# Modulation vectors of a conditioned decoder trunk: the sum on VectorE's free axis in place of partition sums and transposes

## The chip, the cores and the metric

The kernel runs on one core of one Trainium2 chip. The metric is the device time of one execution in microseconds (us); lower is better. Three runs of the kernel before took 1095.26, 1096.6 and 1096.73 us; their median is 1096.6.

## The reference

Two layers work on x, 256 tokens by 1024. Each layer runs a half-step SwiGLU feed-forward (FFN), a token mixer, and a second FFN. Around each of the three, the input is normalised, scaled and shifted, and the output is gated, by vectors that depend on the sequence alone:

```
c_act = silu(c)                                  # c: 1024 numbers
for l in range(2):
    mod = c_act @ w_ada[l] + b_ada[l]            # w_ada[l]: 1024 x 9216
    sh0, sc0, g0, sh1, sc1, g1, sh2, sc2, g2 = split(mod, 9)
    h = rmsnorm(x, norm_g[l, 0]) * (1 + sc0) + sh0
    x = x + 0.5 * g0 * swiglu(h, gate, up, down) # 1024 -> 2816 -> 1024
    h = rmsnorm(x, norm_g[l, 1]) * (1 + sc1) + sh1
    x = x + g1 * token_mix(h, ...)
    h = rmsnorm(x, norm_g[l, 2]) * (1 + sc2) + sh2
    x = x + 0.5 * g2 * swiglu(h, ...)
return rmsnorm(x, final_g)
```

The token mixer is a gated unit, a differential attention and a sparse attention side by side, between an input and an output projection. The change touches how `mod` is computed. All inputs are float32.

## The kernel before, in words

The activations lie with the model axis on the partitions: xT is 128 partitions by 8 chunks by 256 tokens. A projection takes 128 output rows at a time. Its weights (`wst`, 128x1024, 512 KB) come in by DMA from SyncE's queue (SP) and are split in two parts for an exact product: ScalarE (ACT) copies the high part `wh` (L207), VectorE (DVE) subtracts for the rest `wl` (L211). TensorE (PE) multiplies wh by both parts of the activations and wl by one, three products for each of 8 chunks (L219). An FFN runs 22 gate/up tiles (`ps_ws`, two times 24 products each; but for the first FFN, the first two tiles start from x before its norm is known, `ps_wu`) and then 8 down tiles (`ps_dn`, 44 products). The mixer runs its parts in an order written out by hand (MIX_ORDER) for TensorE; elsewhere the framework's planner sets the order on each engine. Each engine runs its queue in order.

A modulation vector m of layer l (9 in each) is made in two halves of 512 columns. The first two vectors of layer 0 are made in the startup by another path (`ada_row`, `ada_col`, L362 to L383), which the change leaves as it is. The other 32 halves go through `ada_half` (L183): four loads of 512 KB on SP, each with 256 rows of the summed axis, two on each partition, by 512 columns; VectorE multiplies by the column of silu(c) and adds into `acc`, 128x512 (L192, L194). That leaves the sum over the 128 partitions, which `ada_flush` (L171) does one step later: four transposes on TensorE into one PSUM bank (L176), four copies on ScalarE that give the sum of each row (L180), and then the bias add and the gain or gate on VectorE (`ada_cols`, L158). The bank (pool `pst`, one buffer) is shared with the norms and the compressed branch. The load buffers (`ad`, four of 4 KB a partition) are shared with the compression weights.

The callers set where halves run (L1016 to L1036): 4 during the gate/up tiles and 4 during the down tiles of the first FFN, 4 in the first mixer (steps `a` of MIX_ORDER and the output projection), 6 and 2 in the next FFN, 6 and 4 in layer 1's first FFN, none in its mixer, and 2 in the last FFN. The first FFN begins with `startup` (L356), where seven gate/up tiles are built up chunk by chunk in seven PSUM banks while the first modulations arrive; it ends with the rest of the constants and parameters being loaded (L440, L441) and the Silu evictions of the seven tiles.

Of the kernel before, what the change touches and what calls it, by code (L numbers as in the profile page):

```python
# [10 lines left out]
F32 = mybir.dt.float32  # L11
# [6 lines left out]
P = 128  # L18
# [27 lines left out]
NW = 16         # products that warm the tensor engine while the first loads arrive  # L46
BUFS = dict(acc=2, ad=4, sm=4, t1k=9, u=27, wh=6, wl=6, wst=5)
LATE = 4        # tiles of the first FFN that run before it loads modulation weights
# order of the parts of the token mixer, layer by layer
# [9 lines left out]
NE = 2          # gate/up tiles (and pairs of w_in tiles) that run before the norm is known  # L59
NS = 7          # gate/up tiles of the first FFN that are accumulated while w_ada arrives  # L60
# [51 lines left out]
def trunk_kernel(ctx: ExitStack, tc: tile.TileContext, A, depth=DEPTH, nf=NF, fsplit=FSPLIT):  # L112
# [33 lines left out]
    nc.scalar.activation(cact, par[:, :8], AF.Silu)  # L146
    ones = sing.tile([P, 1], F32, name="ones")
# [21 lines left out]
    pending = []  # L169

    def ada_flush():  # L171
        while pending:
            l, m, hf, acc = pending.pop(0)
            ps = pst.tile([P, 512], F32, name="ps_ada", tag="st")
            for c in range(4):
                nc.tensor.transpose(ps[:, c * P:(c + 1) * P], acc[:, c * P:(c + 1) * P], ident)  # L176
            red = sm.tile([P, 4], F32, name="red", tag="red")
            for c in range(4):
                junk = tp.tile([P, P], F32, name="junk", tag="t1k")
                nc.scalar.activation(junk, ps[:, c * P:(c + 1) * P], AF.Copy, accum_out=red[:, c:c + 1])  # L180
            ada_cols(l, m, slice(hf * 4, hf * 4 + 4), red)

    def ada_half(l, m, hf):  # L183
        ada_flush()
        acc = accp.tile([P, 512], F32, name="acc")
        for q in range(4):
            st = adp.tile([P, 2, 512], F32, name="ast")
            nc.sync.dma_start(st, A["w_ada"][l, m, hf, q])
            for k2 in range(2):
                col = cact[:, 2 * q + k2:2 * q + k2 + 1]  # L190
                if q == 0 and k2 == 0:
                    nc.vector.tensor_scalar_mul(acc, st[:, 0, :], col)  # L192
                else:
                    nc.vector.scalar_tensor_tensor(out=acc, in0=st[:, k2, :], scalar=col, in1=acc,  # L194
                                                   op0=ALU.mult, op1=ALU.add)
        pending.append((l, m, hf, acc))

# [38 lines left out]
    # brings the table of Sqrt in behind an instruction  # L236
# [5 lines left out]
    # 1/rms of every token, broadcast over the partitions  # L242
# [36 lines left out]
    # x * gain before the norm is known: parts of a chunk, and the shift as two more columns  # L279
# [11 lines left out]
    # W^T (x * gain) and, per row, W^T shift  # L291
# [17 lines left out]
    # out[128 rows of W, T] of W^T h: weights stationary  # L309
# [45 lines left out]
    # the first gate/up tiles, chunk by chunk of the model axis as its modulation arrives  # L355
    def startup(ns):  # L356
# [84 lines left out]
        dma(par[:, npar0:], A["par"][:, npar0:])  # L441
        return [swiglu_mul(ps[:, :T], ps[:, T:], None, None, up, "u") for ps in pss]
# [7 lines left out]
    def ffn(l, w, ada_f, ada_d, nxt):  # L450
# [17 lines left out]
        for f in range(f0, nf):  # L468
            ada_flush()
            for args in slots.get(f - f0 - late, ()):  # L470
                ada_half(*args)
            pg = ws_in(gate[f], psm, "mm")
            pu = ws_in(upw[f], psm, "mm")
            act.append(swiglu(pg, pu))
            for _ in range(2):
                if raw:
                    n = f0 - len(raw)
                    act[n] = act_tile(raw.pop(0))
# [4 lines left out]
        for m in range(KD):  # L483
            ada_flush()
            for args in slots.get(m, ()):
                ada_half(*args)
            if m == KD - 2:
                ada_flush()
                sqrt_table(after)
                if nxt is not None:  # L490
                    u_shift(*nxt)
            ps = psm.tile([P, 2 * T], F32, name="ps_dn", tag="mm")
            final = nxt is None and m == KD - 1
            f0_ = 0
            for n in fsplit:
                wh, wl = split(A["w_down"][l, w, m, :, f0_ * P:(f0_ + n) * P], n * P)
                for j in range(n):
                    f = f0_ + j
                    if final:
                        for n3, (wx, rhs) in enumerate(((wh, act[f][:, :T]), (wh, act[f][:, T:]), (wl, act[f][:, :T]))):  # L500
                            mm(ps[:, :T], wx[:, j * P:(j + 1) * P], rhs, f == 0 and n3 == 0, f == nf - 1 and n3 == 2)
                        continue
                    mm(ps, wh[:, j * P:(j + 1) * P], act[f], start=(f == 0), stop=False)
                    mm(ps[:, :T], wl[:, j * P:(j + 1) * P], act[f][:, :T], start=False, stop=(f == nf - 1))
                f0_ += n
            after = add_out(l, s, m, ps, nxt, 1 if final else 2)

# [22 lines left out]
    # exp of score segments [128, n, keys] in PSUM, with the sums of their rows  # L530
# [13 lines left out]
    def mix(l, ada, nxt):  # L544
# [10 lines left out]
        # lambda of the differential attention, on every partition  # L555
# [29 lines left out]
        # -- projections, tokens on partitions --  # L585
# [31 lines left out]
        # -- gate of the spatial gating unit (before the norm is known) --  # L617
# [8 lines left out]
        # -- blocks of the compressed branch: columns (group, block), position code, position code --  # L626
# [15 lines left out]
        # -- values of the differential attention, v of the gating unit --  # L642
# [22 lines left out]
        # -- differential attention --  # L665
# [93 lines left out]
        # -- spatial gating unit --  # L759
# [35 lines left out]
        # -- compressed keys and values --  # L795
# [40 lines left out]
        # -- sparse attention --  # L836
# [120 lines left out]
        def ada_next():  # L957
            ada_flush()
            if ada:
                ada_half(*ada.pop(0))  # L960
# [44 lines left out]
        ada_flush()  # L1005
        for m in range(2, KD):
            if ada:
                ada_next()
            if m == KD - 2:
                ada_flush()  # L1010
                sqrt_table(after)
                u_shift(*nxt)
            after = w_out(m, 0, KD)

# [66 lines left out]
def _layout(inp, depth, nf):  # L1081
# [5 lines left out]
    o["w_ada"] = g["w_ada"].reshape(depth, 4, 2, P, NMOD, 2, 512).transpose(0, 4, 5, 1, 3, 2, 6)  # L1087
# [54 lines left out]
```

## Time and profile before

| what | value |
|---|---|
| median of three runs | 1096.6 us |
| span of the profiled execution (the page gives no time around it) | 1093.7 us |
| PE busy | 1060.2 us, 97%, 7928 products |
| PE weight loads | 970.2 us, 89% |
| DVE busy | 850.8 us, 78%, 1573 instructions |
| ACT busy | 624.7 us, 57%, 1320 instructions |
| DMA | 257.55 MB, mean 235 GB/s |
| chain that ended last | PE 83%, DVE 10%, ACT 5%, issue 1%, DMA 1% |

Busy times are sums over one execution; engines run side by side. The span goes from the first to the last instruction. Products on PE are pipelined, so that their durations overlap: a product of 283 ns can follow the one before after less than half of that. The chain goes back from the last instruction to what released it, step by step, and shows which engine's work set the end.

### The profile page before, as it was taken

The page shows a single profiled execution, that of the slowest core. Times are in us where ns is not written, and L with a number is a line of the kernel's source. Part 1 is how long each engine was busy: PE and PEld are TensorE (multiplying, and loading weights), DVE is VectorE, ACT ScalarE, POOL GpSimd, SP SyncE. Part 2 cuts the span into 40 slices and gives each one's busy share as a digit, 9 for nine tenths or more (in the row PEclk, how much of TensorE's full clock was granted, in tenths as well). Part 3 has the DMA queues.
Part 4 walks back from the last instruction along what each step waited for, and adds up shares of the span by engine and source line. Part 5 has one row for each costly group of instructions (what it writes and reads, how often), then busy time and mean ns, then how long its engine had stood idle before and what let it go on. Part 6 is the DMA issues. An engine that isn't in the chain of part 4 may idle for free.

```text
span 1093.7 us, 20684 instructions
## 1 busy us (share of the span) xinstructions
PE 1060.2 (97%) x7928; PEld 970.2 (89%) x7928; DVE 850.8 (78%) x1573; ACT 624.7 (57%) x1320; POOL 0.2 (0%) x4
## 2 busy tenths in 40 slices
PE   8999999998988999999999999999999999999997
PEld 5899998887775999999899999988787699999986
DVE  3479999767997999887879878786799878555563
ACT  4365545666675865554556555455867766454441
POOL 0000000000000000000000000000000000000000
PEclk8999999999998999999999999999999999999999
DMA  8868988944835679997866888785555145555551
GB/s 330 295 238 339 355 326 310 324 160 132 320 130 181 221 243 343 341 312 252 280 230 231 318 277 297 263 312 197 180 184 184 58 154 174 188 180 187 174 159 39
DMA packets 73827, 257.55 MB, mean 235 GB/s; under 512 B 8320, under 2 KB 9728, under 8 KB 73728
## 3 DMA queue, kind: packets, MB, share of 16 engines
q1 hardware_dynamic: 73728, 256.23, 67.3%
q8 instruction: 62, 1.02, 0.4%
q14 instruction: 37, 0.30, 0.1%
HBM read 255.14 MB, written 1.05 MB: 234 GB/s over the span
## 4 chain that ended last, share of the span: by engine, by line
PE 83%; DVE 10%; ACT 5%; issue 1%; DMA 1%; SPq 0%; DVEq 0%; ACTq 0%
PE ps_ws L219 41%; PE ps_dn L219 23%; PE ps_wu L219 5%; PE ps_fst L219 4%; PE ps_out L219 4%; DVE wl L211 2%; DVE rt L512 2%; PE ps_y L219 1%; DVE mx L533 1%; ACT cmpa L637 1%; PE ps_ada L176 1%; PE ps_row L219 1%; DVE acc L194 1%; ACT pn L538 1%; DMA ast<-in_w_ada_dram 1%
## 5 line engine op out<-in xcount | busy, mean ns | idle before, releaser
L207 ACT ACTIVATE wh<-wst 128x1024 fp32r<-128x1024 f32 (+2 forms) x332 | 340.3, 1030 | 289.0 <-PE ps_ws L219 101.9
L219 PE MATMUL ps_ws<-h,wh 128*128 128x256 f32 x2720 | 488.9, 283 | 6.9 <-DVE dv L650 6.1
L211 DVE TENSOR_TENSOR wl<-wst,wh 128x1024 fp32r<-128x1024 f32 (+2 forms) x332 | 391.0, 1183 | 118.2 <-ACT wh L207 116.9
L219 PEld LDWEIGHTS ps_ws<-h,wh 128*128 128x128 f32 x2720 | 419.6, 190 | 9.2 <-DVE dv L650 7.0
L219 PE MATMUL ps_ws<-h,wl 128*128 128x256 f32 x1360 | 383.2, 282 | 0.3 <-DVE wl L211 0.3
L219 PEld LDWEIGHTS ps_ws<-h,wl 128*128 128x128 f32 x1360 | 258.0, 190 | 0.5 <-DVE wl L211 0.5
L219 PE MATMUL ps_dn<-act,wh 128*128 128x512 f32 (+1 forms) x726 | 249.1, 391 | 0.0
L219 PE MATMUL ps_dn<-act,wl 128*128 128x256 f32 x704 | 197.7, 281 | 0.0
L194 DVE SCALAR_TENSOR_TENSOR acc<-ast,cact,acc 128x512 f32<-128x512 f32 x224 | 167.3, 747 | 2.5
L219 PEld LDWEIGHTS ps_dn<-act,wh 128*128 128x128 f32 x726 | 134.9, 188 | 30.3
L219 PEld LDWEIGHTS ps_dn<-act,wl 128*128 128x128 f32 x704 | 133.2, 189 | 0.0
L219 PE MATMUL ps_wu<-ut,wh 128*128 128x258 f32 (+1 forms) x320 | 60.1, 286 | 0.9 <-DVE ut L288 0.9
L219 PEld LDWEIGHTS ps_wu<-ut,wh 128*128 128x128 f32 x320 | 49.7, 189 | 1.4 <-DVE ut L288 1.3
L342 DVE TENSOR_TENSOR a<-ps_ws,sg 128x256 f32<-128x256 f32 x75 | 31.6, 421 | 21.8 <-PE ps_ws L219 21.5
L219 PE MATMUL ps_out<-y,wh 128*128 128x256 f32 x256 | 47.4, 286 | 0.2 <-DVE xT L325 0.2
L215 ACT ACTIVATE act<-a 128x256 fp32r<-128x256 f32 x88 | 35.2, 408 | 21.1 <-DVE a L342 19.1
L219 PE MATMUL ps_fst<-h,wh 128*128 128x256 f32 x224 | 43.4, 297 | 1.8 <-ACT h L275 1.8
L219 PE MATMUL ps_wu<-ut,wl 128*128 128x258 f32 x160 | 45.0, 282 | 0.0
L219 PEld LDWEIGHTS ps_fst<-h,wh 128*128 128x128 f32 x224 | 35.5, 198 | 6.9 <-issue 4.5
L219 PEld LDWEIGHTS ps_out<-y,wh 128*128 128x128 f32 x256 | 39.8, 191 | 1.6 <-issue 1.0
L325 DVE SCALAR_TENSOR_TENSOR xT<-ps_dn,hg,xT 128x256 f32<-128x256 f32 x63 | 30.2, 480 | 12.0 <-PE ps_dn L219 11.3
L226 ACT ACTIVATE sq<-xT 128x256 f32<-128x256 f32 x48 | 19.9, 414 | 33.7 <-DVE xT L325 33.2
(203 smaller groups left out, 1115.1 us busy)
## 6 DMA issues: line engine op xcount, KB each, us to landing
ast<-in_w_ada_dram SPq DMA_DIRECT2D x144, 512.0 KB, 5.3
wst<-in_w_gate_dram SPq DMA_DIRECT2D x81, 512.0 KB, 4.5
wst<-in_w_up_dram SPq DMA_DIRECT2D x81, 512.0 KB, 4.3
wst<-in_w_down_dram SPq DMA_DIRECT2D x64, 512.0 KB, 4.5
wst<-in_w_in_ws_dram SPq DMA_DIRECT2D x28, 512.0 KB, 3.8
wst<-in_w_down_dram SPq DMA_DIRECT2D x32, 384.0 KB, 4.0
wst<-in_cmp_w_dram SPq DMA_DIRECT2D x16, 512.0 KB, 5.8
wst<-in_w_out_dram SPq DMA_DIRECT2D x16, 512.0 KB, 4.8
```

Source lines behind the costliest of these rows:

```text
L176: nc.tensor.transpose(ps[:, c * P:(c + 1) * P], acc[:, c * P:(c + 1) * P], ident)
L194: nc.vector.scalar_tensor_tensor(out=acc, in0=st[:, k2, :], scalar=col, in1=acc, op0=ALU.mult, op1=ALU.add)
L207: nc.scalar.activation(wh, st, AF.Copy)
L211: nc.vector.tensor_sub(wl, st, wh.bitcast(F32))
L215: nc.scalar.activation(dst[:, :T], src, AF.Copy)
L219: nc.tensor.matmul(out, lhsT, rhs, start=start, stop=stop, skip_group_check=True)
L226: square = nc.scalar.activation(sq, xT[:, k, :], AF.Square)
L325: nc.vector.scalar_tensor_tensor(out=xT[:, m, :], in0=ps[:, half * T:(half + 1) * T], scalar=hg[l][:, s, m:m + 1], in1=xT[:, m, :], op0=AL ...
L342: nc.vector.tensor_mul(a, pu, sg)
L512: nc.vector.tensor_mul(out, z, t)
L533: nc.vector.tensor_reduce(mx[:, :n], ps, axis=AX.X, op=ALU.max, negate=True)
L538: nc.scalar.activation(pt[:, g * w:(g + 1) * w], ps[:, g, :], AF.Exp, bias=mx[:, g:g + 1], accum_out=su[:, g:g + 1])
```

## The change

The weights w_ada are laid out so that the summed axis of 1024 lies along the free axis: a load of 512 KB now holds 128 modulations on the partitions and all 1024 rows of the sum beside each other. silu(c) is kept as a row on every partition (`crow`, 128x1024), loaded at the end of the startup and put through Silu there. For 128 modulations VectorE runs one instruction, which multiplies the weights by crow (in place) and gives the sum of each partition in one column of `red` (`accum_out`); four of them make a half, and ada_cols follows at once. `ada_flush`, the pending list, the acc tiles of 512 columns, the transposes and ScalarE's copies are gone. The host's layout of w_ada follows, and c is handed over on 128 partitions. Comments that the diff deletes are left out here.

```diff
@@ trunk_kernel
     nc.scalar.activation(cact, par[:, :8], AF.Silu)
+    crow = sing.tile([P, D], F32, name="crow")
...
-    pending = []
-
-    def ada_flush():
-        while pending:
-            l, m, hf, acc = pending.pop(0)
-            ps = pst.tile([P, 512], F32, name="ps_ada", tag="st")
-            for c in range(4):
-                nc.tensor.transpose(ps[:, c * P:(c + 1) * P], acc[:, c * P:(c + 1) * P], ident)
-            red = sm.tile([P, 4], F32, name="red", tag="red")
-            for c in range(4):
-                junk = tp.tile([P, P], F32, name="junk", tag="t1k")
-                nc.scalar.activation(junk, ps[:, c * P:(c + 1) * P], AF.Copy, accum_out=red[:, c:c + 1])
-            ada_cols(l, m, slice(hf * 4, hf * 4 + 4), red)
 
     def ada_half(l, m, hf):
-        ada_flush()
-        acc = accp.tile([P, 512], F32, name="acc")
-        for q in range(4):
-            st = adp.tile([P, 2, 512], F32, name="ast")
-            nc.sync.dma_start(st, A["w_ada"][l, m, hf, q])
-            for k2 in range(2):
-                col = cact[:, 2 * q + k2:2 * q + k2 + 1]
-                if q == 0 and k2 == 0:
-                    nc.vector.tensor_scalar_mul(acc, st[:, 0, :], col)
-                else:
-                    nc.vector.scalar_tensor_tensor(out=acc, in0=st[:, k2, :], scalar=col, in1=acc,
-                                                   op0=ALU.mult, op1=ALU.add)
-        pending.append((l, m, hf, acc))
+        red = sm.tile([P, 4], F32, name="red", tag="red")
+        for c in range(4):
+            st = adp.tile([P, D], F32, name="ast", tag="ast")
+            nc.sync.dma_start(st, A["w_ada"][l, m, hf * 4 + c])
+            nc.vector.scalar_tensor_tensor(out=st, in0=st, scalar=1.0, in1=crow, op0=ALU.mult, op1=ALU.mult,
+                                           accum_out=red[:, c:c + 1])
+        ada_cols(l, m, slice(hf * 4, hf * 4 + 4), red)
@@ startup
         dma(par[:, npar0:], A["par"][:, npar0:])
+        dma(crow, A["crow"])
+        nc.scalar.activation(crow, crow, AF.Silu)
         return [swiglu_mul(ps[:, :T], ps[:, T:], None, None, up, "u") for ps in pss]
@@ ffn, mix: every call of ada_flush() goes
...
@@ _layout
-    o["w_ada"] = g["w_ada"].reshape(depth, 4, 2, P, NMOD, 2, 512).transpose(0, 4, 5, 1, 3, 2, 6)
+    o["w_ada"] = g["w_ada"].reshape(depth, D, NMOD, KD, P).transpose(0, 2, 3, 4, 1)
+    o["crow"] = np.broadcast_to(g["c"][0], (P, D))
```

## Rows read from the trace of the kernel before

**Rows 1.** By stage: us, length, PE, PEld, DVE, ACT, POOL busy, clock, DMA, GB/s.
```profile
70.70:224.00 153.30, 152.99 (x1125) 144.65 (x1125) 138.49 (x210) 87.32 (x180) 0.00 (x0) 1.00 0.86 320
224.00:374.00 150.00, 136.34 (x979) 113.78 (x978) 126.85 (x314) 102.57 (x273) 0.00 (x0) 0.95 0.55 188
374.00:565.00 191.00, 191.00 (x1446) 182.58 (x1445) 164.03 (x259) 105.72 (x206) 0.00 (x0) 1.00 0.83 289
565.00:757.00 192.00, 192.00 (x1455) 183.61 (x1454) 158.72 (x252) 107.24 (x222) 0.00 (x0) 1.00 0.79 270
757.00:897.00 140.00, 133.38 (x979) 113.24 (x978) 115.95 (x289) 99.60 (x243) 0.00 (x0) 0.98 0.44 153
897.00:1086.00 189.00, 188.19 (x1453) 181.56 (x1451) 109.88 (x163) 90.92 (x146) 0.00 (x0) 1.00 0.49 159
```

**Rows 2.** The chain that ended last, its shares by line, whole kernel.
```profile
by line: PE ps_ws L219 41.1%; PE ps_dn L219 22.6%; PE ps_wu L219 4.9%; PE ps_fst L219 3.9%; PE ps_out L219 3.7%; DVE wl L211 1.9%; DVE rt L512 1.6%; PE ps_y L219 1.5%; DVE mx L533 1.4%; ACT cmpa L637 1.4%; PE ps_ada L176 1.3%; issue 1.2%; P
```

**Rows 3.** Chain pieces in feed-forward stages: start us, us, what.
```profile
99.66 0.44 PE ps_ada L176 x4
...
111.92 16.90 PE ps_ws L219 x144
...
915.77 56.32 PE ps_ws L219 x480
972.09 0.44 PE ps_ada L176 x4
```

**Rows 4.** PE timeline round one group of transposes: start us, us, engine, line.
```profile
110.85 0.28 PE L219 MATMUL ps_ws<-h,wl 128*128 128x256 f32 x1
...
111.21 0.28 PE L219 MATMUL ps_ws<-h,wl 128*128 128x256 f32 x1
...
112.00 0.28 PE L219 MATMUL ps_ws<-h,wl 128*128 128x256 f32 x1
```

**Rows 5.** Chain pieces of the transposes in the first mixer.
```profile
345.57 1.04 PE ps_ada L176 x4
...
355.71 0.44 PE ps_ada L176 x4
...
367.72 0.44 PE ps_ada L176 x4
```

**Rows 6.** Groups by line and form: busy us, mean ns | idle before.
```profile
L211 DVE TENSOR_TENSOR wl<-wst,wh 128x1024 fp32r<-128x1024 f32 x286 | 348.0, 1221 | 116.2 <-ACT wh L207 115.0
L207 ACT ACTIVATE wh<-wst 128x1024 fp32r<-128x1024 f32 x286 | 302.0, 1060 | 251.0 <-PE ps_ws L219 91.1 <-issue 84.9 <-PE ps_dn L219 47.1
...
L194 DVE SCALAR_TENSOR_TENSOR acc<-ast,cact,acc 128x512 f32<-128x512 f32 x224 | 167.3, 747 | 2.5
...
L180 ACT ACTIVATION_READ_ACCUMULATOR junk<-ps_ada 128x1 f32 x128 | 26.1, 204 | 0.0
...
L272 DVE SCALAR_TENSOR_TENSOR tn<-xT,gs,rb 128x256 f32<-128x256 f32 x48 | 20.8, 478 | 0.3
...
L192 DVE TENSOR_SCALAR acc<-ast,cact 128x512 f32<-128x512 f32 x32 | 15.4, 482 | 0.4 <-PE ps_ada L176 0.2 <-DMA ast<-in_w_ada_dram 0.2
...
L160 DVE TENSOR_TENSOR mod<-red,par 128x4 f32<-128x4 f32 x32 | 5.0, 157 | 1.3 <-ACT junk L180 1.2
```

**Rows 7.** DVE timeline in the first mixer: start us, us, engine, line.
```profile
288.05 0.74 DVE L194 SCALAR_TENSOR_TENSOR acc<-ast,cact,acc 128x512 f32<-128x512 f32 x1
288.71 1.22 DVE L211 TENSOR_TENSOR wl<-wst,wh 128x1024 fp32r<-128x1024 f32 x1
289.85 0.74 DVE L194 SCALAR_TENSOR_TENSOR acc<-ast,cact,acc 128x512 f32<-128x512 f32 x1
```

**Rows 8.** SP timeline at the end of the startup.
```profile
53.56 0.38 SPq L201 DMA_DIRECT2D wst<-in_w_gate_dram  x1
```

**Rows 9.** ACT timeline at the end of the startup.
```profile
66.68 0.39 ACT L337 ACTIVATE sg<-ps_fst 128x256 f32<-128x256 f32 x1 [1.09 <-PE ps_fst L219]
```

**Rows 10.** Waits, whole kernel: the largest of ACT for weights: us, times, longest.
```profile
ACT wh L207 <- DMA wst<-in_w_down_dram: 4.6, 4, 2.0
```

More of the change, by code (lines that the diff above doesn't have):

```diff
@@ L468, in ffn @@
         for f in range(f0, nf):
-            ada_flush()
             for args in slots.get(f - f0 - late, ()):
@@ L483, in ffn @@
         for m in range(KD):
-            ada_flush()
             for args in slots.get(m, ()):
@@ L487, in ffn @@
             if m == KD - 2:
-                ada_flush()
                 sqrt_table(after)
@@ L957, in ada_next @@
         def ada_next():
-            ada_flush()
             if ada:
@@ L1004, in mix @@
             steps[name](*map(int, args))
-        ada_flush()
         for m in range(2, KD):
@@ L1009, in mix @@
             if m == KD - 2:
-                ada_flush()
                 sqrt_table(after)
```

## The prediction

> **What bounds the kernel now.** I read the stages first, then the chain of waits, then single stretches. The stage table [rows 1] has one row per feed-forward (FFN) or mixer stage behind the startup, which fills the first 70.7 us. In the four FFN rows TensorE (first busy column) is busy for all but 0.3, 0, 0 and 0.8 us of the stage, at full granted clock. VectorE (third column) is the next engine: 138.5 of 153.3 us in the first FFN, 164.0 of 191, 158.7 of 192, 109.9 of 189. In the two mixers TensorE is idle for 13.7 and 6.6 us; the first, which carries modulation work, takes 150 us and the second 140. So in an FFN a microsecond of TensorE work is a microsecond of the kernel, as long as VectorE and the loads keep up; in the first mixer VectorE counts too.
>
> The chain [rows 2] has ps_ada L176, the transposes that the change removes, with 1.3% of 1093.7 us = 14.2 us. Its pieces in the FFNs are 0.44 us each [rows 3]; four transposes make one group. The chip's own order says the same: the two weight products before a group start 0.36 us apart (110.85, 111.21), the two around it 0.79 us (111.21, 112.00) [rows 4], so a group costs 0.43. And 480 weight products without a group take 56.32 us, 0.117 each; 144 between two groups take 16.90, again 0.117 [rows 3]: beside the gap the groups slow nothing.
>
> **Counting.** A half (512 modulations) is one group of four transposes. The code asks for 8 halves in the first FFN, 4 in the first mixer, then 8, 10 and 2 in the other FFNs: 32, of which 28 are in FFNs. 28 x 0.44 = 12.3, and the three groups of the first mixer that are on the chain have 1.04 + 0.44 + 0.44 = 1.9 [rows 5]; together 14.2, the chain's share.
>
> **The change part by part.**
>
> *TensorE.* 128 transposes go: -12.3 us in the FFNs, where nothing else is late by much (below), and -1.9 in the first mixer. The fourth mixer group is not on the chain: 0. The 16 transposes of the startup (L379) stay.
>
> *ScalarE.* 128 copies with sum from PSUM and their 128 accumulator reads (204 ns each [rows 6]) go. ScalarE is busy for 87 of 153 us in its fullest FFN [rows 1] and before its largest group, the copies of the weights (L207), it idles mostly for TensorE [rows 6], so 0. The one PSUM bank that they shared with the norms is free earlier; 0 too.
>
> *VectorE.* Before, a half is one product of 128x512 (482 ns) and seven products with add (747 ns) [rows 6]: 0.48 + 7 x 0.747 = 5.71 us. After, it is four products over 128x1024 that also give a sum. The trace has none with a sum on this engine. The same instruction takes 478 ns for 256 columns and 747 for 512 [rows 6], 1.05 ns a column, so 747 + 2 x 269 = 1285 ns for 1024. Reading the sum out I take as a small instruction of this engine, 157 ns [rows 6]. That gives 4 x (1.285 + 0.157) = 5.77 us, 0.06 more than before: no change. Bounds: from below the plain two-input subtraction of 128x1024, 1221 ns, with a read that hides wholly, 4.88 us a half, 0.83 less; from above twice the time a column, 747 + 512 x 1.05 + 1024 x 1.05 = 2.36 us, with ScalarE's read of 0.204, 10.3 us, 4.5 more. They lie far apart; I take the value next to the row of the same instruction, L194. In the FFNs +0.06 is hidden by VectorE's slack of 14.8 us or more [rows 1]. In the first mixer VectorE runs its instructions end to end, and each starts some 0.08 us before the one before it ends (288.05, 288.71, 289.85 against 0.74 and 1.22 long [rows 7]), for old and new alike: 4 halves x 0.06 = +0.2 us there, with bounds of -3.3 and +18.
>
> Here a rule speaks against the change. The row shows L194 with two f32 inputs and a scalar at 1.05 ns a column [rows 6]. The Trainium skill, "Vector Engine (DVE) Microarchitecture Reference", section "7. Points that are easy to get wrong", says that this instruction runs at half rate when both tensor sources lie in SBUF and are not bf16, since both read ports are then taken and none is left to read back the accumulator. By L194's row it does not hold for the instruction without a sum; no run here shows it with one. The sum by the rule is the second rival below.
>
> *Waits and order.* The bias add of a half now waits for VectorE's own sums alone, no longer for TensorE and ScalarE, and is not put off to the next step: it comes earlier, gain 0. A load buffer is free after one product of 1.2 us instead of two of 0.67: no later, so SP, on which the weight loads queue behind these loads, is not held longer. Bytes and pieces of the modulation loads are the same.
>
> *Startup.* New are one load of 512 KB (c on all partitions) and one Silu over 128x1024. The load is issued on SP ahead of the gate weights that go out at 53.56 [rows 8]; at the 320 GB/s of the next stage [rows 1] it holds them for 1.6 us, and they are not needed before 66.68, when the first tiles are evicted. The Silu waits for that load on ScalarE's queue with the seven Silu evictions behind it, which free the PSUM banks that TensorE needs next. It costs about the 1060 ns of the copy of that shape [rows 6], and ScalarE is idle for 1.09 us just there [rows 9]. So 0 to 1.6 + 1.06 = 2.7; I take 0.3, since both covers are larger than what they cover.
>
> **Sum.** -12.3 - 1.9 + 0.2 + 0.3 = -13.7 us: a span of 1093.7 - 13.7 = 1080.0. The page gives the profiled execution's span alone; the median of the three runs, 1096.6, is 2.9 above it. Forecast 1082.9 us, with 1079.1 (VectorE at its lower bound, -3.5 against its term, and no startup cost) to 1087.2 (startup at its upper bound, +2.4, and the 1.9 us of the mixer's groups not gained) for this case. **Chance 0.70.**
>
> **Rivals.**
>
> *The gain is handed back to VectorE or the loads.* With TensorE faster, the weights' split on VectorE or their loads end last in places. For: DMA share 0.86 and 0.83 in the first and second FFN, VectorE 90% in the first [rows 1]. Against: the largest wait of ScalarE for a weight load is 4.6 us in all over four times [rows 10], and TensorE never stands. If it takes back all 16 groups of these two stages, 16 x 0.44 = 7.0: 1090. **0.09.**
>
> *Half rate with a sum.* One mechanism: the product with sum takes 2.36 us, a half 4 x (2.36 + 0.157) = 10.1, 4.36 more than before. VectorE then needs 138.5 + 8 x 4.36 = 173.4 in the first FFN, 20.1 beyond the stage's length; 198.9 against 191 (+7.9), 202.3 against 192 (+10.3) in the next two; the last keeps its gain (-0.9). The first mixer, without cover, gets 17.4 - 1.9 = +15.5. With 0.3 of startup +53: **1150 us**, slower. It decides from about 1.9 us for product and read: then a half costs 1.9 us more, the mixer 7.6 - 1.9, the first FFN loses its gain, and only 20 x 0.44 = 8.8 is left to balance it. For it: two f32 inputs occupy what reads there is, and no sum has been seen. Against: the full rate of L194 and L272 with the same inputs. By the rule of that page this is the outcome. **0.11.**
>
> *The mixer's order suffers.* An instruction that others wait for can be stuck behind a block of 1.285 instead of 0.747 us on VectorE's in-order queue. 16 blocks in the first mixer, 0.54 more each: 8.6 us if all are hit, 4.3 by half: 1087 to 1091.5. For: VectorE's weight parts, rotary products and row maxima (wl, rt, mx) are on the chain [rows 2]. Against: where the engine has no idle time, its total counts and not the order. **0.07.** Another 0.03 is left for the unforeseen.
>
> **How the numbers follow.** A measurement of this kernel can tell about 0.2%, 2.2 us, from no change: faster is below 1094.4, slower above 1098.8. The first two cases and the mixer's fall below, 0.86 nominally; I give some of that away, since three of the terms rest on one unseen instruction: faster 0.82, same 0.05, slower 0.13. The range reaches from 1078 over the handed-back cases to 1095 and leaves out the half rate.
>
> **What would show it.** In the changed profile: no ps_ada outside the startup, and the 0.44 us gaps between weight products gone; 128 products with sum of about 1.29 us and 128 small reads; VectorE's busy time within 10 us of 850; the FFN stages shorter by about 3.5, 3.5, 4.4 and 0.9 us, the first mixer by 1 to 2; the load and Silu of c done before 67 us with TensorE's start into the weights unmoved. Wrong it is if the product takes over 1.9 us, if TensorE begins to stand in the FFNs, or if the first mixer grows by more than the FFNs shrink.

## The result and the profile after

The changed kernel takes 1102.78 us (median of four runs, 1102.25 to 1103.51), the kernel before 1096.62 beside it. The ratio is 1.0061, 95% interval 1.0046 to 1.0075: slower by 6 us, where 13.7 less was forecast. The profiled execution has a span of 1101.5 us, against 1093.7.

The stages of the changed kernel follow, each cut at TensorE's first product of it, so that the sum has no gaps; the columns are those of [rows 1].

```profile
71.40:219.10 147.70, 146.98 (x1072) 138.51 (x1073) 129.83 (x205) 76.50 (x113) 0.00 (x0) 1.00 0.87 322
219.10:372.90 153.80, 136.90 (x978) 114.00 (x977) 134.96 (x335) 99.79 (x243) 0.00 (x0) 0.96 0.65 219
372.90:563.20 190.30, 188.09 (x1417) 179.64 (x1416) 164.54 (x280) 90.35 (x138) 0.00 (x0) 0.99 0.85 297
563.20:761.20 198.00, 190.60 (x1417) 181.46 (x1416) 139.95 (x214) 100.68 (x148) 0.00 (x0) 0.97 0.71 234
761.20:904.50 143.30, 132.61 (x978) 111.65 (x977) 115.49 (x292) 99.80 (x243) 0.00 (x0) 0.99 0.45 149
904.50:1092.10 187.60, 187.47 (x1438) 180.02 (x1437) 109.17 (x158) 88.55 (x129) 0.00 (x0) 1.00 0.52 161
```

The same cut through the kernels that the argument rests on, in us. [rows 1] were cut at round times, hence the small differences. FFN a.b is feed-forward b of layer a; "end" is what follows the last FFN. Each line is one execution: that of before_acc6 is the slowest of its eight (1105.63 us against a median of 1101.59), that of before_hold the fastest of its seven (1098.72 against 1100.54), so these two lines are compared with the others only roughly. The recorded expectations cut the stages elsewhere (201.0 us for the changed kernel's FFN 0.2, 188.8 for hold's), so their stage lengths differ from the table's.

| kernel | startup | FFN 0.1 | mixer 0 | FFN 0.2 | FFN 1.1 | mixer 1 | FFN 1.2 | end | span |
|---|---|---|---|---|---|---|---|---|---|
| before | 70.75 | 151.05 | 151.95 | 191.30 | 192.05 | 139.80 | 187.45 | 9.35 | 1093.7 |
| after | 71.40 | 147.70 | 153.80 | 190.30 | 198.00 | 143.30 | 187.60 | 9.40 | 1101.5 |
| hold | 69.80 | 147.70 | 150.55 | 185.85 | 187.65 | 144.50 | 186.15 | 9.40 | 1081.6 |
| before_acc6 | 71.40 | 151.10 | 150.90 | 192.95 | 200.55 | 138.40 | 189.00 | 9.60 | 1103.9 |
| hold_tr | 70.40 | 150.35 | 152.80 | 191.25 | 191.80 | 144.55 | 188.65 | 9.40 | 1099.2 |
| hold_12 | 70.25 | 147.55 | 150.95 | 192.55 | 187.25 | 143.15 | 186.20 | 9.50 | 1087.4 |
| hold_dve | 70.35 | 146.60 | 150.90 | 187.25 | 187.65 | 144.45 | 186.40 | 9.40 | 1083.0 |
| before_hold | 68.60 | 151.10 | 152.20 | 191.10 | 192.65 | 143.20 | 188.75 | 9.30 | 1096.9 |

Read the first two lines against each other. The first FFN gained the 3.4 us that its eight groups of transposes were to give. FFN 0.2 gained 1 instead of 3.5; FFN 1.1 lost 5.95 instead of gaining 4.4; the mixers lost 1.85 and 3.5. In the changed kernel TensorE is idle for 2.2 us in FFN 0.2 and 7.4 in FFN 1.1, where [rows 1] show none, and its granted clock in FFN 1.1 is 0.97. That TensorE begins to stand in the FFNs is one of the signs that the forecast named for being wrong.

What was taken out is gone, and the new instruction is cheap. The chain has unbroken runs of weight products where [rows 3] had a 0.44 us group in between (start, us, what):

```profile
72.61 84.52 PE ps_ws L201 x718
...
586.53 112.64 PE ps_ws L201 x960
```

480 of these products take 56.32 us in [rows 3], 960 take 112.64 here: 0.117 each, as before. The groups by form, beside [rows 6]:

```profile
L193 DVE TENSOR_TENSOR wl<-wst,wh 128x1024 fp32r<-128x1024 f32 x286 | 347.9, 1222 | 113.7 <-ACT wh L189 113.4
...
L176 DVE SCALAR_TENSOR_TENSOR ast<-ast,crow 128x1024 f32<-128x1024 f32 x128 | 154.8, 1221 | 26.9 <-DMA ast<-in_w_ada_dram 26.3
...
L176 DVE DVE_READ_ACCUMULATOR ast<-ast,crow 128x1 f32 x128 | 10.7, 83 | 0.0
```

The product with sum takes 1.221 us, as long as the plain subtraction of the same shape, and the reading of the sum 0.083. A half is 4 x (1.221 + 0.083) = 5.22 us against 5.71: VectorE saves half a microsecond a half. The rule of the Trainium skill ("Vector Engine (DVE) Microarchitecture Reference", "7. Points that are easy to get wrong"), half rate for this instruction with two such sources, would have given 2.36 us by the working of the forecast. The trace does not agree with it for this instruction on f32 data in SBUF.

The chain's shares by line, beside [rows 2], show the new thing:

```profile
by line: PE ps_ws L201 33.9%; PE ps_dn L201 16.9%; DMA ast<-in_w_ada_dram 8.5%; PE ps_wu L201 4.8%; PE ps_fst L201 4.0%; DVE wl L193 3.8%; PE ps_out L201 3.6%; DVE ast L176 3.1%; issue 2.8%; ACT cmpa L618 1.3%; DVE rt L493 1.3%; DVE mx L514
```

The landing of modulation loads (`ast<-in_w_ada`) has 8.5% of the whole, 94 us; it was not among the lines of [rows 2]. Twelve of its pieces lie between 423 and 557 us, 4.5 to 7.4 us each, in FFN 0.2. Two passes of the loop that they belong to (the chain, start, us, what; short pieces left out):

```profile
493.49 0.27 SPq L183
...
493.81 0.42 SPq L175
...
494.29 5.62 DMA ast<-in_w_ada_dram
...
499.93 0.04 DVE ast L176
...
501.50 0.55 DVE wl L193
...
502.97 1.21 DVE wl L193
...
504.19 0.33 SPq L183
...
504.57 7.15 DMA ast<-in_w_ada_dram
```

SP issues a weight load (L183) and behind it a modulation load (L175), which lands 5.6 us later; VectorE's product (L176) waits for it; a weight part `wl` (L193) is queued behind the product; it frees a weight buffer for which SP's next load waits; and behind that on SP stands the next modulation load. Here the loop closes in 10 us.

That a wait of VectorE hurts is not shown by its size alone, so look at what VectorE waits for in FFN 0.2 (us, times, longest). After:

```profile
DVE ast L176 <- DMA ast<-in_w_ada_dram: 23.7, 20, 2.5
DVE wl L193 <- ACT wh L189: 0.6, 1, 0.6
```

Before, the same stage:

```profile
DVE wl L211 <- ACT wh L207: 21.7, 19, 1.8
```

Before, VectorE stood 21.7 us for ScalarE's high part `wh`. That is the wait of an engine that has done all it was given: slack. After, that row has shrunk to 0.6, and the 23.7 us for loads have taken its place. VectorE's busy time there is 164.5 us (table of stages above), and 164.5 + 23.7 = 188.2 of 190.3: VectorE, working or standing in its queue, fills the stage, and TensorE begins to wait for it. First in the down tiles (TensorE's timeline; in brackets the idle time before, and for what):

```profile
504.82 0.40 PE L201 MATMUL ps_dn<-act,wh 128*128 128x512 f32 x1
...
505.17 0.40 PE L201 MATMUL ps_dn<-act,wh 128*128 128x512 f32 x1
...
507.76 0.79 PE L201 MATMUL ps_dn<-act,wh 128*128 128x512 f32 x1 [2.08 <-DVE act L198]
...
508.56 0.63 PE L201 MATMUL ps_dn<-act,wh 128*128 128x512 f32 x1
...
509.20 0.63 PE L201 MATMUL ps_dn<-act,wh 128*128 128x512 f32 x1
```

Then at the seam to the next FFN, where the last residual adds on VectorE are late. Busy time in three slices of 5 us (columns as above), then TensorE's largest wait there and the wait of ScalarE behind it:

```profile
565.00:570.00 5.00, 1.70 (x10) 1.08 (x8) 5.00 (x10) 3.33 (x5) 0.00 (x0) 0.92 0.84 295
570.00:575.00 5.00, 0.95 (x4) 0.84 (x4) 4.93 (x10) 1.15 (x3) 0.00 (x0) 0.50 0.96 321
575.00:580.00 5.00, 5.00 (x26) 5.00 (x26) 3.05 (x8) 1.71 (x3) 0.00 (x0) 0.55 0.88 294
```

```profile
PE ps_wu L201 <- ACT ut L269: 6.7, 2, 5.0
...
573.18 0.42 ACT L208 ACTIVATE sq<-xT 128x256 f32<-128x256 f32 x1 [2.85 <-DVE xT L307]
```

ScalarE's `ut` stands behind `sq`, which waits for VectorE's `xT` in its turn. VectorE (third busy column) is full until 575 while TensorE is busy for 1.70 and 0.95 us of five; VectorE's timeline there has modulation products (565.02, 568.42) ahead of the adds `xT` at 572.15. TensorE's clock is granted at 0.50 in the second slice and 0.55 in the third, when it works again: about its lower level (1.2 of 2.4 GHz). The stand and the slow stretch are in FFN 1.1's 198.00 us.

Why so many halves were in FFN 0.2 is to be read from the count of products by stage (instructions of L176, or of L194 before, divided by those of a half). In order FFN 0.1, mixer 0, FFN 0.2, FFN 1.1, mixer 1, FFN 1.2, the code asks for 8, 4, 8, 10, 0, 2 halves. The kernel before ran 8, 4.7, 9.4, 8, 2, 0, the changed one 8, 6.5, 12, 3.5, 2, 0. The halves had moved forward: FFN 0.2 had 12 instead of 9.4, and it moved 297 GB/s where [rows 1] have 289. By these counts the planner sets VectorE's and SP's work not where the code asks for it but earlier; that buffers limit how much earlier is what before_acc6 and after_ad6 below show.

### The profile page after: what moved, and what is told of

Read it like the earlier page. It is cut to its first block, busy times and chain, and to the rows that moved or that the text cites. A ratio compares the mean times of both kernels' runs of the same rounds, so it can differ in the third digit from the quotient of the medians.

```text
span 1101.5 us, 20045 instructions
## 1 busy us (share of the span) xinstructions
PE 1049.3 (95%) x7800; PEld 956.3 (87%) x7800; DVE 831.7 (76%) x1573; ACT 588.4 (53%) x1065; POOL 0.2 (0%) x4
## 4 chain that ended last, share of the span: by engine, by line
PE 68%; DVE 14%; DMA 9%; ACT 4%; issue 3%; SPq 1%; DVEq 0%; ACTq 0%
PE ps_ws L201 34%; PE ps_dn L201 17%; DMA ast<-in_w_ada_dram 9%; PE ps_wu L201 5%; PE ps_fst L201 4%; DVE wl L193 4%; PE ps_out L201 4%; DVE ast L176 3%; ACT cmpa L618 1%; DVE rt L493 1%; DVE mx L514 1%; PE ps_row L201 1%; PE ps_y L201 1%; ACT wh L189 1%; DMA wst<-in_cmp_w_dram 1%
## 5 line engine op out<-in xcount | busy, mean ns | idle before, releaser
L201 PE MATMUL ps_ws<-h,wh 128*128 128x256 f32 x2720 | 483.0, 281 | 9.6 <-DVE dv L631 6.1
L193 DVE TENSOR_TENSOR wl<-wst,wh 128x1024 fp32r<-128x1024 f32 (+2 forms) x332 | 390.9, 1184 | 116.5 <-ACT wh L189 116.1
L189 ACT ACTIVATE wh<-wst 128x1024 fp32r<-128x1024 f32 (+2 forms) x332 | 336.8, 1026 | 242.3 <-issue 118.8
L176 DVE SCALAR_TENSOR_TENSOR ast<-ast,crow 128x1024 f32<-128x1024 f32 x128 | 154.8, 1221 | 26.9 <-DMA ast<-in_w_ada_dram 26.3
L201 PE MATMUL ps_wu<-ut,wh 128*128 128x258 f32 (+1 forms) x320 | 62.3, 293 | 8.2 <-ACT ut L269 6.7
```

Of the source, the lines that this page charges most:

```text
L176: nc.vector.scalar_tensor_tensor(out=st, in0=st, scalar=1.0, in1=crow, op0=ALU.mult, op1=ALU.mult, accum_out=red[:, c:c + 1])
L189: nc.scalar.activation(wh, st, AF.Copy)
L193: nc.vector.tensor_sub(wl, st, wh.bitcast(F32))
L201: nc.tensor.matmul(out, lhsT, rhs, start=start, stop=stop, skip_group_check=True)
```

## The experiments

Theory A: the new arithmetic is sound; without the transposes nothing holds a half back but its load buffers, the halves run ahead, crowd FFN 0.2, and VectorE falls behind in it. Theory B: the form of the product itself is what costs, wherever it runs. Times are medians; ratios are to the kernel before measured beside each (1096.59 us for the first four, 1095.94 for hold_12, after_ad6, before_hold and hold_m1, 1095.87 for the last two).

### hold: the halves kept where the code asks for them

Each modulation load is ordered on SP behind the last weight load that was asked for before it.

```diff
-            nc.sync.dma_start(st, A["w_ada"][l, m, hf * 4 + c])
+            with tc.issue_after(last[0].ins):
+                nc.sync.dma_start(st, A["w_ada"][l, m, hf * 4 + c])
...
-        nc.sync.dma_start(st, src)
+        last[:] = [nc.sync.dma_start(st, src)]
```

> The changed kernel, but on SP each modulation load stands behind the last weight load that the program asked for before it, so that no half can be loaded ahead of its stage (8, 4, 8, 10 and 2 halves by stage, none in the second mixer, in place of 8, 6.5, 12.5, 3 and 2). Theory A (run-ahead): the loss came from halves pulled forward into the first mixer and the second feed-forward stage, where their loads ended last in the chain. Then the second feed-forward stage goes from 201.0 us back to about 187.8 (191.3 before less 8 groups of 0.44), the second mixer from 139.5 to about 136, and the whole to 1082 to 1086 us. Theory B (form of the product): a product of 1.22 us that waits for its load on VectorE's in-order queue stalls the weight splits behind it wherever it stands. Then the stage stays at 196 us or more and the whole at 1097 or more.

1083.61 us (1080.17 to 1087.82), ratio 0.9885 (0.9867 to 0.9904): 13 us faster than before and 19 faster than the changed kernel, with its arithmetic. The halves by stage are 8, 4.75, 8.1, 9.25, 0.75, 1.25. One expectation missed: the second mixer did not get 3.5 us shorter (143.30 to 144.50). VectorE's waits in FFN 0.2:

```profile
DVE wl L196 <- ACT wh L192: 25.6, 27, 1.8
...
DVE ast L179 <- DMA ast<-in_w_ada_dram: 0.4, 1, 0.4
```

The slack is back, the loads are there, and in FFN 0.2 and 1.1 TensorE is again busy for all but 0 and 0.1 us:

```profile
368.05:553.90 185.85, 185.85 (x1416) 178.67 (x1415) 153.59 (x249) 96.89 (x142) 0.00 (x0) 1.00 0.78 277
553.90:741.55 187.65, 187.53 (x1416) 179.62 (x1415) 159.08 (x262) 97.25 (x142) 0.00 (x0) 1.00 0.83 301
```

Theory B falls. FFN 1.1 with 9.25 halves moves 301 GB/s here, more than the 297 that FFN 0.2 moved in the changed kernel, and gains the 4.4 us of the forecast: neither this rate nor the product is what costs.

### before_acc6: the old arithmetic let run ahead

The kernel before with six acc buffers in place of two, nothing else.

```diff
-BUFS = dict(acc=2, ad=4, sm=4, t1k=9, u=27, wh=6, wl=6, wst=5)
+BUFS = dict(acc=6, ad=4, sm=4, t1k=9, u=27, wh=6, wl=6, wst=5)
```

> The kernel before with 6 instead of 2 acc tiles, and nothing else: old arithmetic, old transposes, but halves may run ahead. By stage its loads are then 8, 4.25, 12.75, 5, 1 and 1 halves, nearly those of the changed kernel. Theory A (run-ahead): the second feed-forward stage gets slower by about what the changed kernel lost against its forecast there, 8 to 13 us, and the whole comes to 1102 to 1112 us. Theory B (form of the product): within 3 us of 1096.6, since the products are the old ones.

1101.59 us (1097.99 to 1105.63), ratio 1.0043 (1.0029 to 1.0057). That is just under the 1102 to 1112 expected. Transposes and all, it loses like the changed kernel: halves 8, 5.4, 12.3, 4.3, 2, 0, and VectorE's waits in FFN 0.2 have the same face:

```profile
DVE acc L194 <- DMA ast<-in_w_ada_dram: 14.3, 11, 2.2
DVE wl L211 <- ACT wh L207: 1.8, 4, 0.8
```

The stages FFN 0.2 and 1.1, and the seam between them:

```profile
373.40:566.35 192.95, 191.65 (x1449) 182.98 (x1448) 174.03 (x278) 99.86 (x203) 0.00 (x0) 1.00 0.87 304
566.35:766.90 200.55, 195.73 (x1456) 186.90 (x1455) 145.45 (x227) 109.83 (x226) 0.00 (x0) 0.98 0.72 234
565.00:585.00 20.00, 15.18 (x94) 14.37 (x93) 14.84 (x29) 9.56 (x17) 0.00 (x0) 0.83 0.80 272
```

VectorE: 174.0 busy and 15.0 for loads (0.7 of them on L192) make 189 of 192.95 us; at the seam TensorE is busy for 15.2 of 20 us at a clock of 0.83. So two acc buffers were a brake in the kernel before. That they brake because acc is read last by the transposes, which stand in TensorE's full queue, follows from the code and was not tried by itself; that the brake is the number of acc buffers is shown.

### hold_tr: the transposes put back alone

hold, with four transposes of the constant crow into the `pst` bank for every half; nothing reads them.

```diff
         ada_cols(l, m, slice(hf * 4, hf * 4 + 4), red)
+        ps = pst.tile([P, 512], F32, name="ps_add", tag="st")
+        for c in range(4):
+            nc.tensor.transpose(ps[:, c * P:(c + 1) * P], crow[:, c * P:(c + 1) * P], ident)
```

> The pinned kernel (hold) with four transposes of a constant added on TensorE per half, which nothing reads; the rest is hold. They price the term that the prediction rested on. If 28 groups in feed-forward stages cost 0.44 us each and the mixer's some, it is 12 to 14 us slower than hold. If TensorE's transposes were hidden behind another limit, it is within 4 us of hold.

1101.01 us (1100.77 to 1102.62), ratio 1.0044 (1.0032 to 1.0056): 17.4 more than hold, against 12 to 14 expected. The transposes are worth what the forecast gave them and some 3 us more; the surplus is in FFN 0.2 (+5.4 where 8 x 0.44 = 3.5) and FFN 1.2 (+2.5 where 0.9). It does not lie in the groups: on the chain each of them takes 0.44 in these two stages. It lies in the products between them: in FFN 0.2 the 960 weight products take 113.8 us (112.6 in hold) and the down products 61.6 (60.8), in FFN 1.2 113.3 (112.6) and 62.3 (61.3). Whether the transposes slow them stays open, since hold without a transpose also has 960 weight products that take 114.0, in FFN 1.1.

### hold_late: the start

hold, with the load of c and its Silu asked for two gate/up tiles later.

```diff
-        dma(crow, A["crow"])
-        nc.scalar.activation(crow, crow, AF.Silu)
...
+            if late and f == f0 + 2:
+                nc.sync.dma_start(crow, A["crow"])
+                nc.scalar.activation(crow, crow, AF.Silu)
```

> The pinned kernel (hold) with the load and Silu of c asked for two gate/up tiles later, so that the Silu no longer stands among the seven Silu evictions that end the startup. In the changed kernel TensorE reaches its first stationary weights at 72.6 us against 71.5 before. If that Silu is the reason, they come back to about 71.5 and the whole is 1.1 us below hold; if the load's 512 KB is the reason, the later load only moves the delay and the whole stays with hold.

1082.4 us (1081.31 to 1084.09), ratio 0.9872 (0.9859 to 0.9886): the fastest kernel of the study, but its interval and hold's overlap. In the changed kernel the Silu stands between the evictions, behind the second of the seven (ScalarE's timeline):

```profile
66.45 0.39 ACT L319 ACTIVATE sg<-ps_fst 128x256 f32<-128x256 f32 x1 [1.09 <-PE ps_fst L201]
67.17 0.38 ACT L319 ACTIVATE sg<-ps_fst 128x256 f32<-128x256 f32 x1 [0.33 <-PE ps_fst L201]
67.45 1.05 ACT L425 ACTIVATE crow<-crow 128x1024 f32<-128x1024 f32 x1
```

So it does not lie in the 1.09 us of idle time of [rows 9], where the forecast put it: those are still there ahead of the first eviction. Nor does it hold up all the other five evictions: the fifth and sixth wait for TensorE again. What it makes late is ScalarE's first copy of a weight, `wh`, which stands behind six evictions and the Silu in hold and behind four evictions in hold_late. The startup column can't show the cost, since it varies by more (68.6 to 71.4 in the table), but TensorE's waits between 64 and 75 us do. In hold, then in hold_late:

```profile
PE ps_ws L204 <- ACT wh L192: 1.4, 2, 0.7
...
PE ps_ws L204 <- DVE wl L196: 0.3, 1, 0.3
```

The changed kernel has the two waits for `wh` too. So the Silu among the evictions costs TensorE some 1.1 us, the 1.1 us that were expected if the Silu is the reason, and the medians of the two kernels differ by 1.2.

### hold_12: as many halves in FFN 0.2, evenly spread

hold, with four halves of FFN 1.1 asked for in FFN 0.2.

```diff
-            ffn(l, 0, halves(l, (4, 3, 5)), halves(l, (7, 6)), (l, 1))
+            ffn(l, 0, halves(l, (5,)), halves(l, (7, 6)), (l, 1))
...
-            ffn(l, 1, halves(l, (8,)) + halves(nl, (1, 0)), halves(nl, (2,)), (nl, 0))
+            ffn(l, 1, halves(l, (8,)) + halves(nl, (1, 0, 4, 3)), halves(nl, (2,)), (nl, 0))
```

> As hold (the changed arithmetic, each modulation load issued on SP behind the last weight load asked for before it), but four of the ten halves of layer 1's first FFN are asked for in the second FFN instead: 12 halves there, about as many as the changed kernel ran ahead to, and 6 in layer 1's first. If the loss of the changed kernel lies in the bytes alone (its second FFN moved 299 GB/s over 201.0 us, 60 MB; here 51.9 + 8.4 = 60 MB), this stage grows from 188.8 us to 195 to 201 and the whole from 1083.6 to 1089 to 1094. If it lies in where the planner put the loads on SP (bunched, ahead of weight loads, with VectorE's product waiting for them), the same 12 halves spread and pinned cost little: the stage 188 to 191, the whole 1081 to 1086, VectorE's waits for modulation loads under 6 us (26.3 in the changed kernel).

1088.76 us (1086.1 to 1091.76), ratio 0.9929 (0.9901 to 0.9957): 4.8 us above hold by the ratios, between the two expectations and nearer to the one that blames the crowding itself. FFN 0.2 has 12.25 halves and takes 192.55 us, 6.7 more than in hold; FFN 1.1 stays at 187.25, at full clock:

```profile
368.75:561.30 192.55, 188.42 (x1417) 179.31 (x1416) 171.69 (x290) 96.50 (x142) 0.00 (x0) 1.00 0.86 308
561.30:748.55 187.25, 187.25 (x1417) 179.55 (x1416) 141.25 (x222) 96.99 (x142) 0.00 (x0) 1.00 0.74 256
```

The waits in it are others than in the changed kernel: ScalarE waits for weights (8.4 us for down weights, 5.0 each for gate and up), and TensorE for `wl`; VectorE's waits for modulation loads come to 1.6 us over the whole kernel.

```profile
ACT wh L192 <- DMA wst<-in_w_down_dram: 8.4, 5, 4.8
...
PE ps_ws L204 <- DVE wl L196: 2.6, 2, 1.5
...
PE ps_dn L204 <- DVE wl L196: 1.5, 1, 1.5
```

So twelve halves in one FFN cost 5 to 7 us even when they are spread and pinned. If that cost is in the changed kernel's loss too, which its other kind of waits does not show, the other 13 or so of its 19 us against hold go with where the halves stood (by the table, 10.35 in FFN 1.1 with the seam at its start, 3.25 in the first mixer with its 6.5 halves): in the changed kernel modulation loads are on the chain until 557, up to the seam; here ten of the twelve halves are asked for in the gate/up tiles, VectorE catches up in the down tiles, and TensorE does not stand at the seam.

### after_ad6: more load buffers

The changed kernel with six load buffers for modulation weights in place of four.

```diff
-BUFS = dict(acc=2, ad=4, sm=4, t1k=9, u=27, wh=6, wl=6, wst=5)
+BUFS = dict(acc=2, ad=6, sm=4, t1k=9, u=27, wh=6, wl=6, wst=5)
```

> The changed kernel with six modulation load buffers in place of four, nothing pinned. The planner then puts 13.25 halves in the second FFN (12.75 with four). If the four buffers only give too little lead for loads that are asked for late, VectorE's waits for them fall from 26.3 us to under 12 and the time to 1088 to 1096. If running ahead itself is the loss, as far as the buffers allow, six allow more: 1100 to 1108, second FFN 199 us or more.

1102.42 us (1100.64 to 1104.65), ratio 1.0055 (1.0034 to 1.0076): no gain. VectorE's waits for modulation loads fall only from 26.3 to 23.6 us over the kernel, and the halves run further ahead (by stage 8, 7, 12.5, 2.5, 2, 0). FFN 0.2 and 1.1 take 190.8 and 195.95 us. More buffers are used up by running further ahead, not kept as lead.

### before_hold: the old arithmetic pinned

The edit of hold, on the kernel before.

```diff
-            nc.sync.dma_start(st, A["w_ada"][l, m, hf, q])
+            with tc.issue_after(last[0].ins):
+                nc.sync.dma_start(st, A["w_ada"][l, m, hf, q])
```

> The kernel before (product and add over the partitions, transposes, copies) with its modulation loads pinned on SP in the same way. It completes the square of old and new arithmetic, free and pinned. Before ran ahead by little, so theory A expects the two first layers' FFNs within 2 us of before (the transposes still cost 18 x 0.44 = 7.9 us in the middle two FFNs) and 1093 to 1099 in all, and the new arithmetic alone, hold against this, 11 to 15 us. The rival: the pinning by itself gains, as much with the old arithmetic, 1086 or less. Of the second mixer: if the new arithmetic made the planner's order there worse (hold 140.6 us, before 135.9), this kernel stays near 136; if it is that no half runs in it when they are pinned, it is near 140.

1100.54 us (1098.72 to 1102.1), ratio 1.0039 (1.0028 to 1.005). The rival, that pinning gains by itself, falls: on the old arithmetic it costs 4 us. In the profiled execution 3.4 of them are in the second mixer. Pinned against pinned, the change is worth 1.0039 - 0.9885 = 1.5%, 17 us, more than the forecast's 13.7. And the kernel shows that VectorE may stand for loads without harm as long as it has slack; its waits in FFN 0.2:

```profile
DVE wl L213 <- ACT wh L209: 18.9, 18, 1.8
DVE acc L194 <- DMA ast<-in_w_ada_dram: 11.5, 6, 5.8
```

11.5 us for modulation loads, yet 18.9 of slack remain, TensorE is never idle and the stage takes 191.10 us as before. Over the kernel VectorE stood 26.4 us for modulation loads here, as long as in the changed kernel.

### hold_m1: two halves in the second mixer

hold, with the two halves of FFN 1.2 asked for in the output projection of mixer 1.

```diff
-                mix(l, [], (l, 2))
+                mix(l, halves(l, (8,)), (l, 2))
...
-            ffn(l, 1, halves(l, (8,)), [], None)
+            ffn(l, 1, [], [], None)
```

> As hold, but the two halves of the last FFN are asked for in the second mixer's output projection, where the kernel before ran two. If the second mixer is 4.7 us longer in hold than before because no half runs in it, it falls from 140.6 to about 136 and the whole to 1079. If the order of VectorE's instructions there is the cause, it stays at 140 to 144 (two halves are 10.4 us of VectorE work, in a stage in which it is busy for 106 of 140.6) and the whole is 1083 to 1087, since the last FFN gives nothing back: its VectorE was not full.

1087.65 us (1086.7 to 1089.13), ratio 0.992 (0.9905 to 0.9936): 4 above hold. Two halves ran in mixer 1, and it stays at 144.3 us (144.5 in hold). That it is long because no half runs in it is not borne out. Of the 3.3 us that this kernel's profiled execution is longer than hold's, 1.5 are in the startup and 1.0 in the first mixer, which the edit does not touch.

### hold_dve and hold_dve_late: the products pinned, the loads free

The changed kernel; each product is ordered on VectorE behind the last `wl` asked for before it, and the loads go as the planner wants. hold_dve_late also has the later c of hold_late.

```diff
-            nc.vector.scalar_tensor_tensor(out=st, in0=st, scalar=1.0, in1=crow, op0=ALU.mult, op1=ALU.mult,
-                                           accum_out=red[:, c:c + 1])
+            with tc.issue_after(lastw[0].ins):
+                nc.vector.scalar_tensor_tensor(out=st, in0=st, scalar=1.0, in1=crow, op0=ALU.mult, op1=ALU.mult,
+                                               accum_out=red[:, c:c + 1])
...
-        nc.vector.tensor_sub(wl, st, wh.bitcast(F32))
+        lastw[:] = [nc.vector.tensor_sub(wl, st, wh.bitcast(F32))]
```

> The changed kernel with its modulation loads free, as the planner wants them, but each product with sum pinned on VectorE behind the last weight part (wl) asked for before it. A load can then run ahead only as far as the four buffers reach, one half, and the products don't pile up. If what the changed kernel lost is that VectorE ran products ahead of its own work and stood in them for their loads (26.3 us in 23 times, and 47 us in which ScalarE waited for VectorE's a), this version is near hold: 1081 to 1087, second and third FFN near 186 and 188 us, VectorE's waits for modulation loads under 4 us. If it is the place of the loads on SP, ahead of the weight loads, it stays at 1092 or more with ScalarE waiting for weights' loads over 15 us.

> As hold_dve, with the load of c and its Silu asked for two gate/up tiles later, as in hold_late (1082.4 there against 1083.6 of hold). If the start costs what the bounds of the forecast allow, 1 to 2.7 us, it is that much below hold_dve; if the load and the Silu hide, within 1.5 us of it.

1084.45 us (1082.92 to 1084.76), ratio 0.9892 (0.9876 to 0.9909), and 1083.61 (1081.67 to 1084.14), ratio 0.9886 (0.9871 to 0.9901). Holding back the products alone recovers all, with halves by stage of 8, 4.5, 8.4, 9.5, 0.5, 1.75. VectorE no longer waits for a modulation load at all; in FFN 0.2 of hold_dve it waits for this:

```profile
DVE wl L196 <- ACT wh L192: 29.1, 30, 1.8
```

ScalarE waits for gate and up weights 17 us over that kernel (9 in hold), and it is no slower for it: the loads' own order on SP need not be pinned. The two kernels differ by 0.8 us, within their intervals.

## Why the prediction was wrong

**The step that failed** is the last but one of the parts, "Waits and order": that the bias add "comes earlier, gain 0", that a load buffer is free "no later, so SP ... is not held longer", and with it the premise in "TensorE" that "nothing else is late by much". I followed each edit to what waits for it, but took the place of the halves in the stages as given. It was not: with the transposes went the acc tiles, of which two were a limit on how many halves could be open. before_acc6 shows that loosening this limit alone costs 0.43%; hold and hold_dve show that holding the halves back again turns the changed kernel from 0.61% slower to 1.15 and 1.08% faster. So a step put at 0 was worth 19 us (1102.78 against 1083.61 in hold).

**The rival nearest to it** was "the gain is handed back to VectorE or the loads", which was given 1090, at 0.09. Its mechanism was right in outline (TensorE begins to wait in the FFNs), but its size, all 16 groups of two stages taken back, was taken for the most that could go: a stage in which VectorE is the limit can become longer than before. The argument against it, that the largest wait for a weight load is 4.6 us [rows 10], looked at the wrong wait (in the changed kernel it is 3.6); and the slack that I counted, 14.8 us or more [rows 1], was counted in busy time alone: the 27 us that VectorE had free in FFN 0.2 are gone with its busy time unchanged, since 23.7 us of waiting in its queue moved in.

**TensorE's term** of -12.3 - 1.9 was right, if small. The first FFN fell by 3.35 (forecast 3.5), and in hold FFN 0.2, 1.1 and 1.2 by 5.45, 4.4 and 1.3 (forecast 3.5, 4.4 and 0.9). The reading that "beside the gap the groups slow nothing" rests on the piece of 16.90 in [rows 3]; other pieces of 144 weight products between two groups take 17.09 us. That hold's 1083.61 us lie close to the forecast of 1082.9 is partly luck: against the kernel before, its FFNs gained 14.5 us and not 12.3, and the second mixer took 4.7 back.

**VectorE's term** was off in the favourable direction: 1.221 + 0.083 and not 1.285 + 0.157, so a half is 0.49 shorter and not 0.06 longer, and VectorE's busy time is 831.7 us, 19 less than before, where a value within 10 of 850 was to show the forecast right. Neither the half rate nor the third rival, the longer blocks, is seen in the first mixer: in hold, with the same blocks and 4.75 halves, it takes 150.55 us against 151.95. The 153.8 of the changed kernel go with its 6.5 halves.

**Startup**: +0.65 in the changed kernel, -0.95 in hold with the same edit. The cover named for the Silu was wrong (it runs behind the idle time, not in it). TensorE's waits put its cost at some 1.1 us in place of 0.3, and the pairs hold and hold_late, hold_dve and hold_dve_late differ by 1.2 and 0.8 us; the bound of 2.7 is not seen.

**The second mixer** was costed at nothing, since the code asks for no half in it. It takes 143.1 to 145.0 us in every kernel but before and before_acc6 (139.8, 138.4). TensorE's waits in it that differ, before:

```profile
PE ps_sg L219 <- ACT pn L538: 0.8, 1, 0.8
...
PE ps_cs L219 <- ACT pct L882: 0.5, 1, 0.5
```

and in before_hold, with the old arithmetic:

```profile
PE ps_sg L221 <- DVE ce L868: 2.2, 1, 2.2
...
PE ps_cs L221 <- ACT pct L884: 1.3, 1, 1.3
PE ps_ws L221 <- DVE rt L514: 1.2, 1, 1.2
```

hold has these same three rows to 0.1 us. So the new product is not needed for it: some 3.4 us of waits come in (2.2 + 1.3 + 1.2 for 0.8 + 0.5) with the old arithmetic too, once the modulation work is placed otherwise. They are waits for small steps (the softmax `ce`, the rotary products `rt`), which speaks for another order of them on VectorE; that was not tried by itself. The changed kernel and hold_m1, with two halves there, are as long with other waits: `ps_cs` for `pct` 2.4 us, `ps_ws` for `rt` 1.2 and 1.3. What makes the planner choose so, and how the old order is had with the new product, stays open; hold_m1 excludes the mere absence of halves.

## What to carry to other kernels

A buffer that is released late can be a governor and not only a cost: before you remove the chain behind it, ask what the planner will do with the freedom, and count where the work would then stand, stage by stage. An engine's slack is read from what it waits for: when the wait for its normal supplier (`wl` for `wh`, 21.7 us) turns into a wait for something that was pulled ahead (23.7 us for loads), the slack is spent, even where its busy time is nearly unchanged (164.0 us in [rows 1], 164.5 after). Where a change hands the planner new freedom, pin the work to the place where it was and time that too: here one line of ordering was worth 19 us.

## What was not expected of the hardware

The product of two f32 tensors in SBUF with a sum took 1221 ns for 128x1024, the same as a plain subtraction, and the reading of the sum 83 ns. A stand of TensorE cost more than its length here: behind the one of 2.08 us at 507 its pairs of products start 0.64 us apart (508.56 and 509.20) where it was 0.35 (504.82 and 505.17), at a granted clock of 0.50 from 509 to 511, and at the seam the granted clock is at 0.50 from 570, while TensorE stands, and at 0.55 over the first 5 us of work behind it.
